# The order of the products in a split-float projection: PSUM tile by PSUM tile, lo part of the weights last

## The chip, the cores and the metric

The kernel runs on one core of a Trainium2 chip. The metric is device time in microseconds, from the first to the last instruction and the little that lies around them; the time given for a kernel is the median of its runs.

## The reference

One inference step of a decoder layer with two parallel branches, on a prompt of 1024 tokens and on 8 single sample tokens with 1024 cached positions each (1032 token columns in all, `NT`). Width is 1024, in 16 heads of 64.

```python
h = x * (1 + scale(c)) + shift(c)                       # adaLN
q, k, v, g_att, u, g_ssm, m_att, m_ssm = split(h @ w_in)   # 1024 x 8192
o = stick_breaking(q, k, v)        # A[t,s] = beta[t,s] * prod_{s<j<t} (1 - beta[t,j]), strictly causal
y = ssm(u)                         # 64 groups of 16 channels, 64 complex states each, scan over time
y = gelu(y + d_skip * u);  y = y * sigmoid(y @ w_glu + b_glu);  y_ssm = (y * silu(g_ssm)) @ w_ssm_out
y_att = (o * silu(g_att)) @ w_att_out
merged = sigmoid(m_att) * y_att + sigmoid(m_ssm) * y_ssm
x = LayerNorm(alpha * x + gate(c) * (merged @ w_out))
```

All is float32. Keys, values, final states and the new `x` are outputs.

## The kernel before, in words

**Projections.** Nearly all large products go through `gemm` (L124). An operand is held as two float32r tiles, `hi` (the rounded value) and `lo` (the rest). A projection takes one slab of weights (1024 inputs by 128 outputs) and makes 128 output rows for all 1032 token columns: three PSUM tiles `ps[0..2]` of 344 columns each (`c`), eight blocks of 128 inputs (`t`), three products for each (`i`): weights hi by activations hi, weights hi by activations lo, weights lo by activations hi. That is 72 matmuls (L141), each with its own weight load. The order before: for the first two and the last two values of `t` (`EDGE` is 2) tile by tile, three products for each `t`; for the four in between, at each `t` first the two products with the weights' hi part for all three tiles, then the three with the lo part. So a projection needs `wlo` for its third product, and its tiles end at products 60, 66 and 72. The next projection uses the same three PSUM buffers (`pj`, three of them; in the merge stage six) in the same order, and its first product in each waits until the former content has been copied out.

**Weights.** `Weights.emit` (L101) loads a slab (`w32`), rounds it on ScalarE (`whi`, L108) and subtracts on another engine (`wlo`, L109: VectorE in the first stages, POOL later). There are two buffers of each; the next slab is prepared when a projection takes its own.

**Stream.** `Stream` holds the queue of projections. `one` issues one matmul, and `weave` spreads them between the hand-ordered steps of the other work by a planned clock. `begin` and `head` start two projections ahead, while their operand is still being made. TensorE's order is thus written out by hand; the other engines' instructions are put in order by the scheduler of the framework, by priority and its own timing model, and each engine runs its queue in order. A projection's evacuation (`evac`) is written after its last matmul, one instruction for each of the three PSUM tiles.

**Stages.** (1) Modulation: `h` is made block by block, with the first two projections (`q` and `k` of pair 0) begun in between. (2) Attention, for eight pairs of heads: scores `z` (L654), sigmoids on ScalarE (L655, L656), a scan on VectorE (L665), transposes (L683) and values (L700), with four projections (`q`, `k`, `v`, gate) for the next pair woven in; `Attention.evac` copies out of PSUM into `z32` tiles (L574). (3) State space, for eight blocks of channels `f`: `matrices` (L936, L942), `inputs` (`sps`, L997; copied to `sr` and `si`, L999), the recurrence `recur` on VectorE (L1019 to L1037, result `xs`), `outputs` (`yp`, L1047 and L1048) and `gelu` (ScalarE L1080 to L1084, VectorE L1083 and L1085, the tanh at L1084 waiting for VectorE's L1083); three projections for each block are woven in, one `u` (copied out on ScalarE by `SSM.take`, L970) and two of the gates (`gate_evac`, L1520, and for the SSM gate also `zgate`, L1522). At the same time `SampleAttention` works through the cache of the sample tokens: indirect gathers on POOL (L807) of 2 MB tiles into `s_t`, multiply-adds on VectorE (`s_sc`, L828; values L823). Small VectorE copies (L805, L818, L815) from a recent tile (`k.last`: `u`, `sr`, `gin`, `gh`) pace them. (4) Merge: three chains of eight projections, `glu`, `ssm_out` and `att_out`, where each takes what the one before wrote (`act_g`, `act_s`, `act_a`); late values of the sample attention (`l_t`, L884, L885) run on VectorE beside them, their result `d_o` is needed by the transposes at L1285, and the projections of `att_out` follow. (5) `finish`: the output projection (L1397) and the LayerNorm.

Of the kernel before, what the change touches and what calls it, by code (L numbers as in the profile page):

```python
# [18 lines left out]
NC3, CW = 3, 344  # L19
KT = 8  # L20
# [57 lines left out]
def cs(c):  # L78
    return slice(CW * c, CW * c + CW)


def blk(i, w=128):
    return slice(w * i, w * i + w)
# [37 lines left out]
        return w  # L121


def gemm(k, act, evac, pre):  # L124


    PE = k.nc.tensor
    if pre:
        pre()
    whi, wlo = k.w.get()  # L130
    k.pj.append(k.pj.pop(0))
    ps = [k.pj[0].tile([128, 512], F32, tag="pj", bufs=NC3, name="pj")[:, 0:CW] for _ in range(NC3)]
    a = act() if callable(act) else act
    three = [(c, i) for c in range(NC3) for i in range(2)] + [(c, 2) for c in range(NC3)]
    ends = lambda ts: [(t, c, i) for c in range(NC3) for t in ts for i in range(3)]
    order = ends(range(EDGE)) + [(t, c, i) for t in range(EDGE, KT - EDGE) for c, i in three]
    order += ends(range(KT - EDGE, KT))
    for n, (t, c, i) in enumerate(order):
        ahi, alo = a[t]
        w, x = ((whi, ahi), (whi, alo), (wlo, ahi))[i]  # L140
        PE.matmul(ps[c], w[:, blk(t)], x[:, cs(c)], start=(t == 0 and i == 0), stop=(t == KT - 1 and i == 2))  # L141
        if n == len(order) - 1:
            evac(ps)
        yield


class Stream:
# [5 lines left out]
        self.clock = 0.0  # L153
        self.begun = deque()

    def add(self, act, evac, pre=None):
        self.jobs.append((act, evac, pre))
        self.left += KT * 9 * MM

    def later(self, ns, fn):  # L160
# [6 lines left out]
    def begin(self, n):  # L167

        for _ in range(n):
            self.begun.append([gemm(self.k, *self.jobs.popleft()), 0])  # L170

    def head(self, n):

# [7 lines left out]
    def one(self):  # L181

        if self.cur is None and self.begun:
            self.cur, self.n = self.begun.popleft()
        if self.cur is None:
            if not self.jobs:
                return False
            self.cur, self.n = gemm(self.k, *self.jobs.popleft()), 0
        next(self.cur)
        self.n += 1  # L190
        self.left -= MM
        self.clock += MM
        last = self.n == KT * 9
        if last:
            self.cur = None
            self.k.w.ensure()
        self.due()
        return None if last else True
# [32 lines left out]
def split_act(k, pool, src):  # L231
    hi = pool.tile([128, NT], F32R, tag="hi", bufs=KT, name="ahi")
    lo = pool.tile([128, NT], F32R, tag="lo", bufs=KT, name="alo")
    k.nc.scalar.copy(hi, src)
    k.nc.vector.tensor_tensor(lo, src, hi.bitcast(F32), ALU.subtract)  # L235
    return hi, lo
# [953 lines left out]
class Merge:  # L1190
# [33 lines left out]
    def glu(self):  # L1224
        k, nc = self.k, self.k.nc
        DVE, ACT = nc.vector, nc.scalar
        self.s_guard = self.pool("sets", "left")
        ps = self.s_guard.__enter__()
        self.act_s, held = [], {}

        def pre(f):
            g = self.ld.tile([128, NT], F32, tag="x", bufs=2, name="g")
            hi, lo = self.act_g[f]
            nc.gpsimd.tensor_tensor(g, hi.bitcast(F32), lo.bitcast(F32), ALU.add)
            s = self.load(k.d_sg[f], "m")
            (nc.gpsimd if GS == "p" else DVE).tensor_tensor(s, g, s, ALU.mult)
            held[f] = s

        def evac(f, p):
            g = held.pop(f)  # L1240
            for c in range(NC3):
                t = self.ld.tile([128, 512], F32, tag="sig", bufs=2, name="sig")[:, 0:CW]
                ACT.activation(t, p[c], AF.Sigmoid, bias=self.bg[:, f:f + 1])
                DVE.tensor_tensor(g[:, cs(c)], g[:, cs(c)], t, ALU.mult)
            self.act_s.append(split_act(k, ps, g))
            k.late.pace(g)

        for f in range(KT):
            k.stream.add(self.act_g, lambda p, f=f: evac(f, p), lambda f=f: pre(f))

    def ssm_out(self):
        k, nc = self.k, self.k.nc
        held = {}

        def pre(f):
            held[f] = self.load(k.d_mm[f], "m")

        def evac(f, p):
            m = held.pop(f)
            for c in range(NC3):  # L1260
                nc.vector.tensor_tensor(m[:, cs(c)], p[c], m[:, cs(c)], ALU.mult)
            k.q["P"].dma_start(k.d_pa[f], m)
            k.late.pace(m)

        for f in range(KT):
            k.stream.add(self.act_s, lambda p, f=f: evac(f, p), lambda f=f: pre(f))

    def open_a(self):

# [21 lines left out]
    def att_out(self):  # L1291
        k, nc = self.k, self.k.nc
        DVE = nc.vector
        self.m_guard = self.pool("setm", "left")
        pm = self.m_guard.__enter__()
        k.act_m, held = [], {}

        def pre(f):
            held[f] = self.load(k.d_ma[f], "m"), self.load(k.d_pa[f], "x")

        def evac(f, p):
            m, a = held.pop(f)
            for c in range(NC3):
                DVE.tensor_tensor(m[:, cs(c)], p[c], m[:, cs(c)], ALU.mult)
            DVE.tensor_tensor(m, m, a, ALU.add)
            k.act_m.append(split_act(k, pm, m))

        for f in range(KT):
            k.stream.add(lambda: self.act_a, lambda p, f=f: evac(f, p), lambda f=f: pre(f))

    def open_gate(self):
        k, io, ld = self.k, self.io, self.ld
# [406 lines left out]
```

## Time and profile before

| what | value |
|---|---|
| median of 3 runs | 1613.56 us (1612.72 to 1615.05) |
| the profiled execution | 1617.42 us, its span 1615.7 us |
| mean granted TensorE clock in it | 0.969 |
| matmuls, of these in projections (L141) | 9321, 6336 |
| start of the state-space stage, of the merge's first products | about 713 us, about 1172 us |
| projections done, start of the output products | 1504.5 us |

In the profile, PE is TensorE's matmuls and PEld its weight loads, DVE is VectorE, ACT ScalarE, POOL GpSimd, SP the queue that issues most DMAs. L141 is line 141 of the kernel. A row of waits reads: who waited <- for whom: microseconds in total, how often, the longest. In a timeline, a bracket at the end of a row is the idle time before that instruction and what ended it. The ends of matmuls are modelled; pace is read from their starts.

### The profile page before, as it was taken

To read this page: it belongs to the slowest core of one execution; us is meant where nothing else is said; L and a number is where in the kernel's file an instruction comes from. 1 tells how busy PE (TensorE), PEld (TensorE's weight loads), DVE (VectorE), ACT (ScalarE), POOL (GpSimd) and SP (SyncE) were. 2 spreads that over 40 slices of the span, in tenths; PEclk is the share of its full clock that TensorE was granted. 3 is DMA by queue.
4 is the path that set the end of the run, shared out by engine and by line. 5 is a ranking of instruction groups with operands and counts; after the bars stand their busy time and mean duration, and the time that the engine had idled before them with its cause. 6 is when DMAs were issued, how large, how long until landed. Compare 5 with 4: busy or idle time off the path is not lost.

```text
span 1615.7 us, 25524 instructions
## 1 busy us (share of the span) xinstructions
PE 1489.5 (92%) x9321; PEld 1410.2 (87%) x9321; DVE 1218.9 (75%) x1717; ACT 736.5 (46%) x1360; POOL 911.0 (56%) x744
## 2 busy tenths in 40 slices
PE   8899999999999999999989978889979786999997
PEld 4789999999999998999888978889779685899885
DVE  5558888888888888743899978787489975744566
ACT  3557777777776776643433333333432212311200
POOL 1738787878777877766566555552176541132164
PEclk9899999999999999999999989999989997999999
DMA  9323433334343434348789887875546677954322
GB/s 356 111 82 89 104 100 97 99 97 113 87 113 93 115 88 111 101 123 288 246 266 287 265 265 249 285 235 132 164 158 222 213 249 261 348 180 140 118 79 91
DMA packets 176731, 275.47 MB, mean 170 GB/s; under 512 B 46395, under 2 KB 119867, under 8 KB 176477
## 3 DMA queue, kind: packets, MB, share of 16 engines
q1 hardware_dynamic: 150555, 180.40, 36.6%
q0 software_dynamic: 23456, 84.95, 16.4%
q10 hardware_dynamic: 2594, 8.49, 2.0%
q8 instruction: 73, 1.20, 0.3%
q14 instruction: 53, 0.43, 0.1%
HBM read 196.77 MB, written 66.24 MB: 163 GB/s over the span
## 4 chain that ended last, share of the span: by engine, by line
PE 49%; DVE 26%; DMA 9%; issue 5%; ACT 3%; POOL 2%; SPq 1%; DVEq 0%; ACTq 0%; POOLq 0%
PE pj L141 32%; PE f L1397 6%; DVE s_sc L828 4%; PE o L700 3%; PE z L654 3%; PE tp L683 3%; DVE ke L665 3%; DVE l_t L884 2%; DMA s_t<-in_cache_k,s_idx 2%; DVE be L666 2%; DVE vs L636 2%; DMA l_t<-in_cache_v,l_idx 2%; DVE l_acc L885 2%; DVE wlo L109 1%; DVE xs L1037 1%
## 5 line engine op out<-in xcount | busy, mean ns | idle before, releaser
L141 PE MATMUL pj<-ahi,whi 128*128 128x344 f32 x2112 | 695.4, 331 | 36.8 <-ACT u L970 17.5
L141 PE MATMUL pj<-alo,whi 128*128 128x344 f32 x2112 | 686.1, 326 | 7.9 <-DVE alo L1220 4.1
L141 PE MATMUL pj<-ahi,wlo 128*128 128x344 f32 x2112 | 581.6, 328 | 6.0 <-POOL wlo L109 6.0
L141 PEld LDWEIGHTS pj<-ahi,whi 128*128 128x128 f32 x2112 | 405.6, 192 | 45.9 <-ACT u L970 18.3
L141 PEld LDWEIGHTS pj<-alo,whi 128*128 128x128 f32 x2112 | 405.6, 192 | 11.9 <-DVE alo L235 4.9
L141 PEld LDWEIGHTS pj<-ahi,wlo 128*128 128x128 f32 x2112 | 382.6, 192 | 8.0 <-POOL wlo L109 6.5
L665 DVE TENSOR_TENSOR_SCAN ke<-ke,eye 128x896 f32<-128x896 f32 (+7 forms) x128 | 217.7, 1701 | 92.4 <-ACT ke L655 92.2
L109 POOL TENSOR_TENSOR wlo<-w,whi 128x1024 fp32r<-128x1024 f32 x53 | 141.6, 2672 | 207.7 <-ACT whi L108 178.8
L108 ACT CAST whi<-w 128x1024 fp32r<-128x1024 f32 x90 | 94.9, 1055 | 137.3 <-PE pj L141 100.1
L655 ACT ACTIVATE ke<-z,nhb 128x448 f32<-128x448 f32 (+2 forms) x192 | 111.8, 582 | 81.1 <-PE z L654 79.2
L666 DVE TENSOR_TENSOR be<-be,ke 128x896 f32<-128x896 f32 (+7 forms) x128 | 128.0, 1000 | 13.0 <-ACT wthi L686 0.5
L828 DVE SCALAR_TENSOR_TENSOR s_sc<-s_t,s_q,s_sc 128x512 f32<-128x512 f32 x126 | 114.0, 905 | 18.0 <-DMA s_t<-in_cache_k,s_idx 12.0
L656 ACT ACTIVATE be<-z,hb 128x448 f32<-128x448 f32 (+2 forms) x192 | 110.6, 576 | 0.0
L807 POOL DMA_INDIRECT s_t<-in_cache_k,s_idx x64 | 70.6, 1103 | 50.8 <-DVE s_sc L828 15.5
L683 PE MATMUL tp<-ident,be 128*128 128x128 f32 x576 | 88.9, 272 | 0.0
L493 POOL TENSOR_TENSOR pt<-tab 128x256 f32<-128x256 f32 x64 | 79.5, 1241 | 3.1
L492 POOL TENSOR_TENSOR pr<-tab 128x256 f32<-128x256 f32 x32 | 25.9, 811 | 89.4 <-DMA tab<-d_tab 78.7
L1520 ACT ACTIVATE gate<-pj 128x344 f32<-128x344 f32 x72 | 32.7, 458 | 95.4 <-PE pj L141 86.5
L109 DVE TENSOR_TENSOR wlo<-w,whi 128x1024 fp32r<-128x1024 f32 x37 | 62.5, 1689 | 15.4 <-ACT whi L108 15.3
L686 ACT CAST wthi<-tp 128x512 fp32r<-128x512 f32 x96 | 56.7, 590 | 32.3 <-PE tp L683 29.9
L654 PE MATMUL z<-kl,qs 128*128 128x448 f32 (+2 forms) x192 | 66.0, 344 | 4.0 <-DMA kl<-kl 4.0
L687 DVE TENSOR_TENSOR wtlo<-tp,wthi 128x512 fp32r<-128x512 f32 x96 | 65.3, 680 | 5.7 <-ACT wthi L686 5.7
(314 smaller groups left out, 2758.5 us busy)
## 6 DMA issues: line engine op xcount, KB each, us to landing
w<-in_w_in SPq DMA_DIRECT2D x38, 512.0 KB
w<-in_w_in POOLq DMA_DIRECT2D x26, 512.0 KB, 5.6
wc<-in_w_cond SPq DMA_DIRECT2D x24, 512.0 KB
d_a<-ox SPq DMA_DIRECT2D x128, 64.0 KB
gst<-d_gg SPq DMA_DIRECT2D x8, 576.0 KB
x<-in_xr SPq DMA_DIRECT2D x9, 512.0 KB
xt<-in_xt SPq DMA_DIRECT2D x8, 516.0 KB
d_sg<-gate SPq DMA_DIRECT2D x8, 516.0 KB
```

The source lines that it names most:

```text
L108: nc.scalar.copy(whi, w32)
L109: self.eng.tensor_tensor(wlo, w32, whi.bitcast(F32), ALU.subtract)
L141: PE.matmul(ps[c], w[:, blk(t)], x[:, cs(c)], start=(t == 0 and i == 0), stop=(t == KT - 1 and i == 2))
L493: POOL.tensor_tensor(t1, c, d, ALU.mult)
L654: nc.tensor.matmul(z[:, 0:wide], st["q", h][:, blk(i)], x[:, s:s + wide], start=j == 0, stop=j == 1)
L655: nc.scalar.activation(ke[:, s:s + cw], z[:, 0:cw], AF.Sigmoid, bias=k.nhb[:, hd:hd + 1], scale=-0.125)
L656: nc.scalar.activation(be[:, s:s + cw], z[:, 0:cw], AF.Sigmoid, bias=k.hb[:, hd:hd + 1], scale=0.125)
L665: nc.vector.tensor_tensor_scan(rev, rev, self.eye[:, NP - n:][:, ::-1], 0.0, ALU.mult, ALU.add)
L666: nc.vector.tensor_tensor(be, be, ke[:, 1:n + 1], ALU.mult)
L683: PE.transpose(tp[:, 2 * order[a] + e], w[e][:, blk(2 * j + a)], k.ident)
L828: DVE.scalar_tensor_tensor(sc, t, q[:, d - d0:d - d0 + 1], sc, op0=ALU.mult, op1=ALU.add)
L1397: PE.matmul(pp[c], a[:, token(i)], w[:, blk(c, 512)], start=(t == 0 and a is ah and w is wh), stop=(t == KT - 1 and a is al))
```

## The change

`gemm` gets a further argument, `fresh`. Without it, the order is: for each of the three PSUM tiles in turn, the sixteen products with the weights' hi part over all eight `t`, then the eight with the lo part. With it, the order is the former one. Fresh are the two projections that `begin` starts in the modulation, and the first (`f == 0`) of `glu`, `ssm_out` and `att_out`. All other projections (attention from `v` of pair 0 on, `u`, the gates, seven of eight in each merge chain) take the new order. The number of matmuls, their operands and their place among the other steps are the same.

```diff
-def gemm(k, act, evac, pre):
+def gemm(k, act, evac, pre, fresh):
...
     order = ends(range(EDGE)) + [(t, c, i) for t in range(EDGE, KT - EDGE) for c, i in three]
     order += ends(range(KT - EDGE, KT))
+    if not fresh:
+        order = [(t, c, i) for c in range(NC3) for part in ((0, 1), (2,)) for t in range(KT) for i in part]
     for n, (t, c, i) in enumerate(order):
...
-    def add(self, act, evac, pre=None):
-        self.jobs.append((act, evac, pre))
+    def add(self, act, evac, pre=None, fresh=False):
+        self.jobs.append((act, evac, pre, fresh))
...
-            self.begun.append([gemm(self.k, *self.jobs.popleft()), 0])
+            self.begun.append([gemm(self.k, *self.jobs.popleft()[:3], True), 0])
...
-            k.stream.add(self.act_g, lambda p, f=f: evac(f, p), lambda f=f: pre(f))
+            k.stream.add(self.act_g, lambda p, f=f: evac(f, p), lambda f=f: pre(f), f == 0)
...
-            k.stream.add(self.act_s, lambda p, f=f: evac(f, p), lambda f=f: pre(f))
+            k.stream.add(self.act_s, lambda p, f=f: evac(f, p), lambda f=f: pre(f), f == 0)
...
-            k.stream.add(lambda: self.act_a, lambda p, f=f: evac(f, p), lambda f=f: pre(f))
+            k.stream.add(lambda: self.act_a, lambda p, f=f: evac(f, p), lambda f=f: pre(f), f == 0)
```

## The prediction

> **What bounds the kernel now.** The profiled execution took 1617.42 us (span 1615.7); the median of the three plain runs is 1613.56, so terms counted in its trace are taken off the median. Two times closer than about 0.2% (3.2 us) can't be told apart here. I read the page's busy shares first, then TensorE's waits, then busy time by stage, then the timelines around the longest waits.
>
> ```profile
> PE 1489.5 (92%) x9321; PEld 1410.2 (87%) x9321; DVE 1218.9 (75%) x1717; ACT 736.5 (46%) x1360; POOL 911.0 (56%) x744
> ...
> PE pj L141 <- ACT u L970: 17.5, 4, 8.7
> PE otp L1285 <- DMA orow<-d_o: 17.2, 1, 17.2
> PE yp L1048 <- DVE xs L1037: 9.9, 4, 3.5
> PE pj L141 <- POOL wlo L109: 6.0, 2, 3.1
> PE pj L141 <- ACT gate L1520: 4.2, 1, 4.2
> PE pj L141 <- ACT z L574: 2.4, 1, 2.4
> PE pj L141 <- ACT zgate L1522: 1.1, 1, 1.1
> ```
>
> TensorE is 92% busy. Of what it waits for, the change can touch two things: a PSUM tile that ScalarE has not yet copied out (`u`, `gate`, `zgate`: 17.5 + 4.2 + 1.1 = 22.8 us) and the weights' lo part (6.0 us). The 2.4 us behind `z` is the start of the third projection, behind the two begun ones, which keep their order; it stays. Now busy time by stage (columns: stretch, its length, PE, PEld, DVE, ACT, POOL busy, granted clock, DMA share, GB/s):
>
> ```profile
> 808.00:841.80 33.80, 28.87 (x187) 27.28 (x185) 32.06 (x56) 11.34 (x23) 22.64 (x18) 0.95 0.77 241
> 841.80:888.10 46.30, 43.18 (x288) 41.78 (x288) 45.19 (x92) 17.02 (x34) 31.65 (x31) 1.00 0.93 302
> 888.10:940.00 51.90, 43.19 (x288) 41.79 (x288) 43.53 (x84) 17.03 (x34) 29.39 (x30) 0.94 0.87 283
> 940.00:989.00 49.00, 44.88 (x288) 43.75 (x288) 39.87 (x79) 17.05 (x34) 26.21 (x26) 0.95 0.76 244
> 989.00:1026.50 37.50, 33.34 (x204) 32.03 (x204) 35.75 (x72) 13.16 (x24) 19.37 (x18) 0.91 0.80 247
> 1087.40:1143.00 55.60, 50.02 (x281) 43.19 (x281) 35.40 (x81) 16.96 (x34) 14.89 (x11) 0.91 0.54 138
> 1181.00:1347.00 166.00, 132.26 (x782) 130.31 (x782) 147.50 (x166) 33.62 (x45) 88.98 (x51) 0.89 0.66 219
> 1347.00:1504.50 157.50, 153.37 (x929) 149.58 (x930) 85.85 (x98) 37.53 (x38) 34.96 (x12) 0.98 0.66 224
> ```
>
> All of the 22.8 us lie in the state-space stage, one per channel block. There VectorE is as full as TensorE (45.19 of 46.30 us and 32.06 of 33.80, but 39.87 of 49.00 later), and the DMA engines are 76 to 93% busy. In the merge, 1181 to 1347, VectorE has 147.50 of 166 us. Only after 1347 is TensorE alone the bound, with hardly a wait. So an idle microsecond of TensorE is worth a microsecond only where VectorE too stands still for it.
>
> **The change, part by part.** *Number and pace of products.* None is added or dropped: 72 in each projection in both orders. The new order puts 24 in a row into one PSUM tile. Rows that bound this: 600 in the old mixed order, and, in the last token block, 24 in a row into one tile of 512 columns against the interleaved tiles before it (columns: PE, PEld).
>
> ```profile
> 1410.07 94.46 PE pj L141 x600
> ...
> 1543.90:1554.90 11.00, 11.00 (x49) 8.85 (x49) 1.00 0.42 145
> 1593.90:1604.90 11.00, 11.00 (x49) 8.72 (x47) 1.00 0.14 52
> ```
>
> 94.46 / 600 = 157 ns each; and 49 products in 11 us either way, so the row of one tile costs nothing.
>
> *PSUM release.* Before, the three tiles end at products 60, 66 and 72, and the next projection rewrites each 12 products later: 12 x 0.157 = 1.9 us. After, they end at 24, 48 and 72 and are rewritten 48 products later, 7.5 us. A copy may be 5.6 us later than now without stopping TensorE. The longest case, in ScalarE's timeline, then TensorE's:
>
> ```profile
> 927.67 0.63 ACT L1084 ACTIVATE gq<-gq 128x512 f32<-128x512 f32 x1 [6.80 <-DVE gq L1083]
> 937.90 0.63 ACT L1084 ACTIVATE gq<-gq 128x512 f32<-128x512 f32 x1 [7.87 <-DVE gq L1083]
> 939.23 1.38 ACT L970 COPY u<-pj 128x344 f32<-128x344 f32 x2
> 940.39 1.07 ACT L108 CAST whi<-w 128x1024 fp32r<-128x1024 f32 x1
> ...
> 930.70 0.62 PE L997 MATMUL sps<-ug,gin 128*128 128x136 f32 x4
> 940.04 0.66 PE L141 MATMUL pj<-ahi,whi 128*128 128x344 f32 x1 [8.72 <-ACT u L970]
> ```
>
> The `u` copies stand behind two tanh that wait for VectorE. In the new order the first tile is done some 10 us before 930.7 (48 products, and a set of `yp` and one of `sps` between them), so about 921: its copy runs there, or right after the tanh of 927.67, both in time. The second is done about 926; if its copy falls behind the tanh of 937.90 it ends near 938.5 and is wanted at 930.9 + 24 x 0.157 + 0.45 = 935.1: a wait of at most 3.4 us in place of 8.7. The other five (1.1 to 4.2 us) are shorter than 5.6 and go. I take 22.8 - 1.7 (half of 3.4) = 21 us of TensorE waits removed.
>
> *What that is worth.* The clock after each wait, then VectorE's timeline in the same places:
>
> ```profile
> 940.00:944.30 4.30, 4.26 (x15) 0.50 0.75 250
> 944.30:948.60 4.30, 4.30 (x30) 0.99 0.53 154
> 888.10:891.50 3.40, 3.36 (x20) 1.00 1.01 267
> 989.00:992.20 3.20, 3.16 (x11) 0.51 1.03 382
> 1087.40:1091.00 3.60, 3.60 (x13) 0.55 0.96 268
> ...
> 838.93 0.69 DVE L1083 TENSOR_TENSOR gq<-gq,gh 128x512 f32<-128x512 f32 x1 [1.04 <-ACT gq L1082]
> 936.40 0.75 DVE L828 SCALAR_TENSOR_TENSOR s_sc<-s_t,s_q,s_sc 128x512 f32<-128x512 f32 x1 [5.46 <-DMA s_t<-in_cache_k,s_idx]
> 946.64 0.15 DVE L805 COPY s_t<-sr 128x1 f32<-128x1 f32 x1 [0.61 <-ACT sr L999]
> 950.57 0.69 DVE L1020 TENSOR_TENSOR gq<-sr,es 128x512 f32<-128x512 f32 x1 [3.78 <-ACT sr L999]
> 996.39 2.29 DVE L838 TENSOR_TENSOR_SCAN s_ke<-s_ke,zcol 128x1024 f32<-128x1024 f32 x1 [1.22 <-ACT s_ke L835]
> 1093.88 0.15 DVE L815 COPY s_acc<-sr 128x1 f32<-128x1 f32 x1 [2.91 <-ACT sr L999]
> 1098.58 0.69 DVE L823 SCALAR_TENSOR_TENSOR s_t<-s_t,s_sc 128x512 f32<-128x512 f32 x1 [3.81 <-DMA s_t<-in_cache_v,s_idx]
> ```
>
> After the waits of 8.7, 4.1 and 4.2 us TensorE ran at half clock for 4.3, 3.2 and 3.6 us: another 2.2 + 1.6 + 1.6 = 5.4 us of its time (after the 3.1 us one it stayed at 1.00). So up to 28 us of TensorE's time comes free. But the stage is handed on by VectorE's recurrence (L1019 to L1037), and VectorE stood still for TensorE only in these rows: 1.0 us at 838.9; 0.6 + 3.8 at 946 and 950, where `sr` waited for `sps` products stuck behind the 8.7 us; 1.2 at 996; 2.9 at 1093.9, of which I count nothing, since at 1098.6 it waits for a gather anyway. Sum 1.0 + 4.4 + 1.2 = 6.6, rounded to 7 with a little from the 2.9. The rest comes back as waits of `yp` for `xs`, 9.9 us now.
>
> *The lo part last.* The first product that needs `wlo` moves from third to seventeenth: 14 x 0.157 = 2.2 us. The two waits, 6.0 us together, shrink to about 1.6. Both lie in the merge before 1347, where VectorE is full and the 17.2 us wait for `d_o` follows: that wait grows by what is saved. Worth 0 at the end; if the cover were gone, 4.4.
>
> *Queues.* No DMA issue is moved. The `whi` buffer is last read at product 64 instead of 71, so the next cast on ScalarE, and the POOL subtraction with the gathers queued behind it, may start up to 1.1 us earlier; POOL's subtraction still waits for the old `wlo`, whose last use stays at 72. I count 0, between 0 and -1. The first copy writes its SBUF tile (`z32`, `gate`, `uu`) 5.6 us earlier; if the former content still has to go out, the copy stands at the head of ScalarE's queue and holds what is behind it (third rival).
>
> *Fresh projections.* The two begun at the start and the first of each merge product keep their order: 0.
>
> Sum: -7 us of 1613.56, that is 1606.5. It lies nearer VectorE's 6.6 than TensorE's 28 because the stage's own rows show VectorE at 95 to 98% in two of the stretches.
>
> **The rivals.** *First: TensorE sets the end after all.* The chain that ended last:
>
> ```profile
> PE 49%; DVE 26%; DMA 9%; issue 5%; ACT 3%; POOL 2%; SPq 1%; DVEq 0%; ACTq 0%; POOLq 0%
> ...
> 939.23 0.77 ACT u L970
> ```
>
> TensorE has half of it, the `u` copy of the longest wait stands on it, and earlier `sps` let gathers (paced on `sr` and `u`) start earlier too. Then all 28 us count, perhaps less one or two: 1587. Against it stand 45.19 of 46.30 us and the DMA share of 0.93.
>
> *Second: nothing moves.* Either VectorE and the gathers take up everything (at 936.40 it waits 5.46 us for a gather that no PSUM tile delays), or the copies stay where they are, behind the tanh, so that the first tile is still free only at 939.9. ScalarE's rows show it working strictly in order: `u` at 939.23 had been ready for 8 us. The Trainium skill says the same, in "TensorE: Matmul & The Clock Gate", Part 1: ScalarE and VectorE are strict first in, first out; by that rule a tile done earlier is free earlier only if its copy is queued earlier, and the trace agrees. Time 1613.5.
>
> *Third, slower: the earlier copies hold ScalarE in the attention stage.* There ScalarE already stands at copies whose products are not done:
>
> ```profile
> ACT z L574 <- PE pj L141: 16.2, 22, 2.0
> ```
>
> That is 0.74 us each time, for tiles that end close together. With tiles 24 products apart, two more copies in each of some 28 projections may stand like this: 28 x 2 x 0.74 = 41 us of ScalarE time, in front of the sigmoids that feed VectorE's scans. ScalarE has slack, so I let a third arrive: +14, 1627. It decides from 0.12 us per added stop that reaches the end (7 us over 56).
>
> The Trainium skill has a rule for the clock as well ("TensorE: Matmul & The Clock Gate", Part 1): an idle window of about 3.4 us halves it. The rows agree (1.00 after 3.1 us, 0.50 to 0.55 after 4.1 and more). By it the removed waits also bring back the half-clock stretches, which are in the first rival's 28 us.
>
> **How the numbers follow.** Forecast, 4 to 14 us faster: 0.50. First rival, 1582 to 1599: 0.13. Second: 0.22. Third: 0.15. Faster by over 0.2% (below 1610.3): 0.50 + 0.13 less 0.03 at the forecast's edge = 0.60; within: 0.25; slower: 0.15. The predicted time is the forecast's, 1606.5; its own range is 1599 to 1610. The range for 8 in 10 leaves out the far half of the first rival and of the third: 1593 to 1619.
>
> **What would show it.** Right: in TensorE's waits `u`, `gate` and `zgate` fall from 22.8 us to under 5, `wlo` from 6.0 to under 2, `yp <- xs` grows above 9.9, the wait for `d_o` stays or grows; products still come every 157 ns; the first `u` copy stands ahead of a tanh in ScalarE's timeline; the handover near 1143 comes about 7 us earlier, and from there to the end the trace is as long as before. Wrong: the waits gone and the handover 20 us earlier (first rival), or the waits still there (second), or the attention stage, 90 to 713, longer by more than 3 us (third).

## The result and the profile after

The changed kernel takes 1632.85 us (median of 4 runs, 1631.98 to 1637.48) beside 1614.3 us for the kernel before on the same chip (1612.72 to 1617.32): a ratio of 1.0118, 95% interval 1.0096 to 1.0139. It is slower by about 19 us, where the forecast was 7 us faster. The two profiled executions differ by less, 14.6 us (spans of 1615.7 and 1630.3), because the one before was some 3 us above its median.

In the changed file all line numbers behind `gemm` are three higher: L144 is the product of a projection, L569 the copy `zg`, L609 the subtraction `kl`, L657 the score product, L1051 `yp`. First the steps of the two profiled executions (us, from marks read off TensorE's timeline: first projection product, last score `z`, first transpose of the state space, last `ysp`, first `otp`, first `f`, end), with four of the experiments beside them:

| step | before | after | `gold` | `klvec` | `gvec` | `gvec_before` |
|---|---|---|---|---|---|---|
| attention stage | 676.2 | 704.1 | 674.3 | 658.1 | 660.8 | 656.8 |
| handover to the state space | 34.0 | 41.5 | 42.4 | 41.8 | 35.0 | 35.2 |
| state space | 409.9 | 395.4 | 395.9 | 394.3 | 396.3 | 405.9 |
| merge, to `otp` | 204.2 | 198.9 | 201.7 | 197.9 | 198.4 | 201.3 |
| merge, to `f` | 157.2 | 155.6 | 154.9 | 153.9 | 153.7 | 153.7 |
| rest | 111.4 | 111.4 | 111.4 | 111.4 | 111.4 | 111.4 |

The change did shorten the stages it was costed in: state space by 14.5 us, merge by 5.3 + 1.6. It lengthened the two steps ahead of them, attention by 27.9 and the handover by 7.5. TensorE's waits after (the columns are who waits for whom, total us, times, longest):

```profile
PE z L657 <- ACT be L659: 35.6, 7, 5.6
PE yp L1051 <- DVE xs L1040: 19.0, 6, 7.8
PE otp L1288 <- DMA orow<-d_o: 11.5, 1, 11.5
PE pj L144 <- POOL wlo L109: 7.1, 2, 5.5
PE pj L144 <- ACT gate L1523: 5.2, 1, 5.2
PE pj L144 <- ACT zgate L1525: 1.2, 1, 1.2
```

The `u` waits (17.5 us) are gone. The new first row is a score product that waits 5 us for ScalarE's sigmoid, seven times: once in each pair of heads but the first. The row in which `zg` occurs before, and then what ScalarE itself waited for after:

```profile
POOL sg L567 <- ACT zg L566: 57.8, 8, 23.6
```

```profile
ACT zg L569 <- POOL kl L609: 32.4, 7, 5.1
ACT zgate L1525 <- POOL gate L1527: 6.1, 1, 6.1
ACT z L577 <- PE pj L144: 9.6, 22, 0.5
```

Before, `zg` appears as something that others wait for, and no row has it waiting. After, it waits seven times for `kl`, which neither feeds it nor is fed by it. The reason is a buffer. `zg` takes its SBUF tile from the tag `z32`, whose three buffers go round as q, k, v, `sg`, `zg`, so `zg` lands in the buffer that holds this pair's keys. Their second half is still to be read by POOL's `kl`, which is held back until the scores of the former pair are out. ScalarE's timeline at the second pair, then POOL's, then TensorE's:

```profile
169.08 0.47 ACT L568 ACTIVATE sg<-pj 128x344 f32<-128x344 f32 x1
174.32 0.45 ACT L569 COPY zg<-pj 128x344 f32<-128x344 f32 x1 [4.77 <-POOL kl L609]
174.66 0.69 ACT L658 ACTIVATE ke<-z,nhb 128x512 f32<-128x512 f32 x1
...
169.58 1.47 POOL L495 TENSOR_TENSOR pi<-tab 128x256 f32<-128x256 f32 x1
171.01 0.80 POOL L496 TENSOR_TENSOR pt<-tab 128x256 f32<-128x256 f32 x1
171.89 2.40 POOL L609 TENSOR_TENSOR kl<-z,kh 64x1024 fp32r<-64x1024 f32 x1
...
175.99 0.80 PE L657 MATMUL z<-kh,qs 128*128 128x512 f32 x1 [5.24 <-ACT be L659]
```

`zg`'s wait of 4.77 us ends when `kl` is done; the sigmoid `ke`, which has nothing to do with either, stands behind it and starts only at 174.66; TensorE waits 5.24 us for the sigmoids' PSUM tiles. The same place before, ScalarE then POOL:

```profile
169.59 0.69 ACT L655 ACTIVATE ke<-z,nhb 128x512 f32<-128x512 f32 x1 [0.39 <-PE z L654]
180.08 0.46 ACT L565 ACTIVATE sg<-pj 128x344 f32<-128x344 f32 x1
180.42 0.45 ACT L566 COPY zg<-pj 128x344 f32<-128x344 f32 x1
...
169.63 3.13 POOL L606 TENSOR_TENSOR kl<-z,kh 64x1024 fp32r<-64x1024 f32 x1
```

`kl` ended 1.5 us earlier then (172.76 against 174.29), still later than 169.55, where `zg` began to wait after the change; `zg` came 8 us after it had ended. In this stage the products of a projection are woven between other work, so "36 products earlier" is not 5.6 us but 11 us (180.08 against 169.08).

The wait costs more than its length. TensorE's clock behind it (stretch, length, PE, PEld, DVE, ACT, POOL busy, granted clock):

```profile
175.99:179.30 3.31, 3.31 (x12) 3.12 (x13) 2.42 (x3) 2.40 (x5) 2.72 (x4) 0.50 0.72 166
179.30:184.00 4.70, 4.70 (x31) 4.39 (x31) 4.00 (x5) 2.74 (x7) 0.00 (x0) 0.85 0.70 172
```

The granted clock stays at half up to 180.74, for 4.75 us. Behind the seven waits such stretches are 2.8 to 6.2 us long, 32.4 us in all, and TensorE is busy throughout them: a loss of at most 16.2 us. Over the same 600 us of the attention stage, before and after:

```profile
90.00:690.00 600.00, 581.43 (x3946) 567.35 (x3946) 505.64 (x480) 427.18 (x860) 440.81 (x375) 1.00 0.38 100
```

```profile
90.00:690.00 600.00, 563.62 (x3753) 552.24 (x3753) 460.49 (x457) 413.10 (x820) 410.70 (x360) 0.96 0.36 95
```

TensorE is idle for 581.43 - 563.62 = 17.8 us more, not for the whole 35.6 us of new waits, because its waits for VectorE in this stretch fell at the same time, from 17.6 us to 0.8. With the half clock that is at most 34 us. Counted by work, the 193 matmuls fewer are 29 us at the former pace of 600 us for 3946; the stage grew by 27.9.

The handover repeats it with another reader. The gates begun there use `z32` too, and the second waits for POOL's multiplication of the first, which stands behind the table products. After, ScalarE then POOL:

```profile
739.00 0.45 ACT L1525 COPY zgate<-pj 128x344 f32<-128x344 f32 x1 [6.10 <-POOL gate L1527]
...
735.93 0.72 POOL L497 TENSOR_TENSOR pi<-pi,pt 128x256 f32<-128x256 f32 x1
736.61 2.35 POOL L1527 TENSOR_TENSOR gate<-gate,zgate 128x1032 f32<-128x1032 f32 x1
```

### The profile page after: what moved, and what is told of

It is laid out like the page before. It is cut to its first block, busy times and chain, and to the rows that moved or that the text cites. A ratio compares the mean times of both kernels' runs of the same rounds, so it can differ in the third digit from the quotient of the medians.

```text
span 1630.3 us, 25533 instructions
## 1 busy us (share of the span) xinstructions
PE 1496.3 (92%) x9321; PEld 1420.3 (87%) x9321; DVE 1191.8 (73%) x1717; ACT 747.1 (46%) x1360; POOL 892.6 (55%) x744
## 4 chain that ended last, share of the span: by engine, by line
PE 53%; DVE 16%; DMA 10%; POOL 9%; issue 5%; ACT 2%; SPq 1%; DVEq 0%; POOLq 0%; ACTq 0%
PE pj L144 35%; PE f L1400 6%; DVE s_sc L831 5%; PE o L703 3%; PE z L657 3%; PE tp L686 3%; POOL pt L496 2%; DMA out_k_p<-sv 2%; DMA s_t<-in_cache_k,s_idx 2%; POOL pr L497 1%; DMA l_t<-in_cache_v,l_idx 1%; POOL kl L609 1%; DVE xs L1040 1%; DMA d_g<-yy 1%; DMA sga<-d_sa 1%
## 5 line engine op out<-in xcount | busy, mean ns | idle before, releaser
L144 PE MATMUL pj<-ahi,whi 128*128 128x344 f32 x2112 | 694.2, 332 | 18.7 <-ACT ahi L237 9.0
L144 PE MATMUL pj<-alo,whi 128*128 128x344 f32 x2112 | 683.9, 327 | 9.4 <-DVE alo L1223 4.0
L144 PEld LDWEIGHTS pj<-ahi,whi 128*128 128x128 f32 x2112 | 407.6, 193 | 26.6 <-ACT ahi L237 9.5
L144 PE MATMUL pj<-ahi,wlo 128*128 128x344 f32 x2112 | 420.9, 326 | 7.1 <-POOL wlo L109 7.1
L144 PEld LDWEIGHTS pj<-alo,whi 128*128 128x128 f32 x2112 | 407.5, 193 | 13.9 <-DVE alo L238 6.7
L144 PEld LDWEIGHTS pj<-ahi,wlo 128*128 128x128 f32 x2112 | 349.1, 191 | 9.4 <-POOL wlo L109 7.6
L668 DVE TENSOR_TENSOR_SCAN ke<-ke,eye 128x896 f32<-128x896 f32 (+7 forms) x128 | 213.0, 1664 | 62.8 <-ACT ke L658 62.6
L109 POOL TENSOR_TENSOR wlo<-w,whi 128x1024 fp32r<-128x1024 f32 x53 | 133.0, 2510 | 225.2 <-PE pj L144 125.1
L831 DVE SCALAR_TENSOR_TENSOR s_sc<-s_t,s_q,s_sc 128x512 f32<-128x512 f32 x126 | 111.5, 885 | 14.6 <-DMA s_t<-in_cache_k,s_idx 13.0
L657 PE MATMUL z<-kh,qs 128*128 128x448 f32 (+2 forms) x192 | 68.4, 356 | 35.6 <-ACT be L659 35.6
L810 POOL DMA_INDIRECT s_t<-in_cache_k,s_idx x64 | 70.1, 1095 | 54.2 <-DVE s_q L821 14.6
L570 POOL TENSOR_TENSOR sg<-sg,zg 128x1032 f32<-128x1032 f32 x8 | 24.1, 3018 | 102.0 <-ACT zg L569 102.0
L495 POOL TENSOR_TENSOR pr<-tab 128x256 f32<-128x256 f32 x32 | 31.7, 990 | 85.4 <-DMA tab<-d_tab 72.3
```

What stands on the lines that cost most here:

```text
L109: self.eng.tensor_tensor(wlo, w32, whi.bitcast(F32), ALU.subtract)
L657: nc.tensor.matmul(z[:, 0:wide], st["q", h][:, blk(i)], x[:, s:s + wide], start=j == 0, stop=j == 1)
L668: nc.vector.tensor_tensor_scan(rev, rev, self.eye[:, NP - n:][:, ::-1], 0.0, ALU.mult, ALU.add)
L831: DVE.scalar_tensor_tensor(sc, t, q[:, d - d0:d - d0 + 1], sc, op0=ALU.mult, op1=ALU.add)
```

## The experiments

Theory A: an evacuation that comes early writes an SBUF buffer that POOL has still to read, and holds ScalarE's queue. Rivals: every early copy costs ScalarE by itself (theory B), or TensorE's long rows into one PSUM tile disturb the stage (theory C). All of these ran beside the kernel before; its median was 1617.0 us beside `gold`, `only_g`, `only_qkv` and `klfirst`, 1613.1 beside `klvec`, `best`, `only_ssm` and `only_merge`, 1612.2 beside `klvec_before`, `klvec_tile` and `gvec`, and 1613.8 beside `gvec_before`.

**Attention's gate in the former order, all else new (`gold`).**

```diff
-            S.add(k.act_h, lambda ps, kind=kind: box[0].evac(p, kind, ps))
+            S.add(k.act_h, lambda ps, kind=kind: box[0].evac(p, kind, ps), None, kind == "g")
```

> The changed kernel, but the attention gates (kind g, once per pair) keep the former order. Theory A: the loss is the early copy zg, which takes the z32 buffer that still holds the keys, and stands at the head of ScalarE's queue until POOL's subtraction kl has read them; then the seven waits of z for the sigmoids be (35.6 us) and the half clock after them go, the attention stage is as long as before within 3 us, and with the gain of the later stages the time is about 1596 (1591 to 1602). Theory B: the loss is that every earlier copy (q, k, v, g) holds ScalarE while its products are not done; then about a quarter of the 36 us goes, and the time is 1620 to 1626. Theory C: the long rows of one PSUM tile themselves disturb the attention stage; 1620 to 1630.

Measured: 1607.09 us, ratio 0.9939 (0.9923 to 0.9956). Eight projections of the kernel make the difference between slower and faster, and the time is below what theories B and C gave (1620 and more). TensorE's wait for the sigmoids falls from 35.6 us to this row:

```profile
PE z L657 <- ACT be L659: 4.7, 3, 2.4
```

The number forecast, 1596, was missed: the handover stays at 42.4 us, which the forecast had let go with the rest, and the merge is 2.8 us longer than after the change.

**Only attention's gate new (`only_g`), and only q, k and v of attention new (`only_qkv`).** The same argument of `add` is set to `kind != "g"` or `kind == "g"`, and to `True` in all other projections.

> The former order everywhere, except the attention gates (kind g), which take the new one. Theory A: the whole loss of the attention stage is here, 32 to 37 us: 1646 to 1652. Theory B: a quarter of it: 1622 to 1626. Theory C: a quarter: 1620 to 1626.

> The former order everywhere, except q, k and v of the attention stage, which take the new one. Theory A: within 3 us of the kernel before, 1611 to 1617, or a little below, as short waits for late VectorE work may change. Theory B: three quarters of the loss, 1638 to 1644. Theory C: the same, 1635 to 1644.

Measured: 1636.27 us, ratio 1.0120 (1.0103 to 1.0137), and 1620.98 us, 1.0021 (1.0001 to 1.0040). The eight gate projections alone bring a loss as large as the whole change's, though without its gains: their attention stage is 699.3 us, which is 23.1 of the 27.9 us. With q, k and v alone it is 675.2 us, no longer than before, where theories B and C gave three quarters of the loss; the whole is 0 to 6 us slower. The size that theory A gave for the gates was 10 us too large. With the gates alone, `zg` waits:

```profile
ACT zg L569 <- POOL kl L609: 22.9, 7, 3.9
```

**The subtraction `kl` with a higher priority (`klfirst`).** The POOL instruction is put under `high_priority(HURRY)`.

> The changed kernel with one edit: the subtraction kl on POOL gets the same high priority as the copies out of PSUM, so that it goes ahead of the table products in POOL's queue; all orders of products stay new. Theory A: kl ends some us earlier, the key's z32 buffer is free when zg comes, the wait of zg for kl (32.4 us) falls below 8 us, and the time is 1597 to 1608. Theories B and C: no change, 1628 to 1637.

Measured: 1634.13 us, ratio 1.0105 (1.0082 to 1.0128). It decides nothing, since the edit did not move the instruction. POOL's timeline, with the table product still ahead:

```profile
172.51 0.80 POOL L496 TENSOR_TENSOR pt<-tab 128x256 f32<-128x256 f32 x1
173.39 2.40 POOL L610 TENSOR_TENSOR kl<-z,kh 64x1024 fp32r<-64x1024 f32 x1
```

**The subtraction `kl` on VectorE, new order throughout (`klvec`).**

```diff
-        nc.gpsimd.tensor_tensor(kl[own], z[own, 0:NP], kh[own].bitcast(F32), ALU.subtract)
+        nc.vector.tensor_tensor(kl[own], z[own, 0:NP], kh[own].bitcast(F32), ALU.subtract)
```

> The order after throughout, but the subtraction that makes the keys' lo part (kl) runs on VectorE instead of POOL, so that it no longer stands behind POOL's table products. Theory A: the copy zg then waits below 8 us for kl over the stage (32.4 after), TensorE's waits of z for ScalarE's be fall from 35.6 to below 12 us, the attention stage falls from 704 to about 682 us, and the time to 1606 to 1616 us; VectorE does some 14 more subtractions of 1 to 1.3 us, which can cost up to 9 us of this. Rival B (the early copy costs ScalarE by itself, whoever reads the buffer): attention stays above 698 us and the time above 1627 us.

Measured: 1586.78 us, ratio 0.9852 (0.9824 to 0.9879): 46 us less than after the change by the medians, 43 by the ratios, by moving the one instruction that `zg` waited for. The row of `zg` waiting for `kl` is gone, `zg` runs where its product ends, and TensorE hardly stands:

```profile
PE z L657 <- ACT be L659: 3.5, 8, 1.0
```

```profile
167.59 0.47 ACT L568 ACTIVATE sg<-pj 128x344 f32<-128x344 f32 x1
167.94 0.46 ACT L569 COPY zg<-pj 128x344 f32<-128x344 f32 x1
```

The early copy doesn't hold ScalarE by itself: the rival, an attention stage above 698 us, is refuted. But the attention stage is 658.1 us, 18 us shorter than before the change, and the time 19 us below the 1606 to 1616 forecast; theory A doesn't give that. So the next run takes the order away again.

**The former order with `kl` on VectorE (`klvec_before`).**

> The former order everywhere, with the subtraction kl on VectorE: the order is the one difference to the kernel that has kl on VectorE and the new order (1586.8 us; its attention stage 658, handover 42, state space 394, the two merge steps 198 and 154). Theory A with a separate gain of moving kl (the new order is worth +7.5 us at the handover, -14.5 in the state space, -5 in the merge, nothing in the attention stage once POOL doesn't read the buffer late): attention 656 to 663 us, total 1595 to 1603. Rival F (the attention stage needs the new order for its 658 us): attention 670 to 677 us, total 1608 to 1616.

Measured: 1588.35 us, ratio 0.9853 (0.9833 to 0.9874). The attention stage is 655.5 us, and the total is 7 us below the range that theory A gave: most of the gain of `klvec` is the moved subtraction's own, in either order. It also leaves the new order worth nothing that can be told (1586.78 against 1588.35): by the profiles, its state space is 12.4 us shorter (394.3 against 406.7) and its merge 3.7, but its handover is 7.7 longer, its attention stage 2.6, the last part of its merge 1.8, and its first product starts 3.1 us later.

**The state-space gates.** In `best`, attention's gates and the state-space gates of kind g keep the former order (the argument of `add` is `s == "g"`); `kl` stays on POOL. In `gvec`, all is new, `kl` is on VectorE, and so is the gate's multiplication:

```diff
-            nc.gpsimd.tensor_tensor(t, t, z, ALU.mult)
+            nc.vector.tensor_tensor(t, t, z, ALU.mult)
```

> The order after, but the eight projections of the attention's own gate and the eight state-space gates whose second copy feeds a POOL product (kind g) keep the former order. Theory A (an early copy into an SBUF buffer that POOL still has to read holds ScalarE): the step from the last scores to the first transpose of the state space, 42.4 us when only the attention's gate keeps the former order, falls back to about 34 us, the waits of zgate for POOL fall from 18.8 us to below 8, and the rest stays: 1599 us (1594 to 1604). Rival D (the handover is long because the u copies come early, not the gates): the step stays near 42 us and the time near 1607 us.

> kl on VectorE, the new order, and the multiplication of the state-space gate by its sigmoid on VectorE instead of POOL, so that the buffers of the three gates made at the handover come free without POOL's table products ahead. Theory A at the second place: the handover falls from 41.8 to 34 to 37 us, ScalarE's waits for POOL's gate (17.2 us) go. Whether the time follows: 1577 to 1582 us if those 6 us last, 1584 to 1589 us if the merge stage gives them back, as it did where the gates alone went back to the former order.

Measured: `best` 1607.61 us, ratio 0.9973 (0.9957 to 0.9989); `gvec` 1581.74 us, ratio 0.9809 (0.9787 to 0.9831). In both the handover falls as theory A says, 42.4 to 34.9 and 41.8 to 35.0 us, so its place is confirmed twice, once by a later copy and once by an earlier reader; `best` also refutes rival D, since its `u` copies still come early. Only `gvec` keeps the gain: the time of `best` is no better than `gold`'s and missed its forecast of 1599. In `best` the merge takes 208.8 us instead of `gold`'s 201.7, with these waits there (`gold` has 14.1 us for `d_o`):

```profile
PE otp L1288 <- DMA orow<-d_o: 17.8, 1, 17.8
PE pj L144 <- POOL wlo L109: 11.8, 4, 6.3
```

Why the merge gave it back in one and not in the other was not settled. `gvec` is the fastest version of all, 50 us below the changed kernel.

**The former order with both operations on VectorE (`gvec_before`).**

> The former order everywhere, with both POOL operations that read the shared buffers (kl and the gate's multiplication) on VectorE: beside the kernel with both on VectorE and the new order (1581.7 us; handover 35, state space 396, merge 198 and 154) it gives what the order by itself is worth once nothing holds the early copies. My forecast's arithmetic (some 20 us of waits removed, most given back as waits for VectorE, a net of 7 us): 1586 to 1591 us. Rival H (the multiplication on VectorE brings the 5 to 6 us whatever the order): 1580 to 1584 us, and the order is worth nothing.

Measured: 1590.08 us, ratio 0.9845 (0.9821 to 0.9870). Against `gvec` the order is now worth 8.3 us by the medians and 5.8 us by the ratios (0.0036 of 1614); the two intervals overlap by 0.001, so a small gain is likely rather than sure. In the former order the multiplication on VectorE brings nothing (1590.08 against 1588.35), so what `gvec` gained over `klvec` (5 us by the medians, 6.8 in the handover) goes to the collision. TensorE's waits, `gvec_before` then `gvec`:

```profile
PE otp L1285 <- DMA orow<-d_o: 16.8, 1, 16.8
PE pj L141 <- ACT u L970: 15.3, 3, 7.3
PE yp L1048 <- DVE xs L1037: 7.1, 4, 2.4
```

```profile
PE yp L1051 <- DVE xs L1040: 19.0, 6, 6.5
PE otp L1288 <- DMA orow<-d_o: 10.0, 1, 10.0
```

15.3 us of waits for `u` go, and 11.9 us come back as waits of `yp` for VectorE's recurrence.

**The stages one at a time (`only_ssm`, `only_merge`).** Only the state space's u and gate projections new; only the merge's three.

> The former order in all of the attention's and the merge's projections, the new one in the u and gate projections of the state space alone. Theory A: attention as before (676 us), handover 41.5 instead of 34.0 us, state space near 395 instead of 410 us, merge as before: 1607 to 1611 us on a chip where before takes 1615. Rival E (the state space's gain comes out of the time that the attention stage lost, as work that was done there earlier): the state-space step stays above 404 us and the time is 1619 to 1625 us.

> The former order everywhere but in the three projections of the merge stage (their first tile row each keeps its own setting). If the merge's gain of 5 us in the order after is its own: 1609 to 1612 us where before takes 1615, with the step between the state space's output and the last output transpose near 199 us instead of 204. If it comes from what the state-space stage left undone or done: 1614 to 1616 us and 203 to 205 us.

Measured: 1606.4 us, ratio 0.9963 (0.9947 to 0.9978), with a state space of 395.6 and a handover of 40.9 us; and 1613.76 us, ratio 1.0015 (1.0002 to 1.0029), with a merge of 207.7 us to `otp`. The state space's gain and the handover's loss both belong to the state-space projections. The merge step is longer than either forecast for it (199, or 203 to 205). The merge's 5 us after the change are not the merge order's own.

**The lo part not last (`klvec_tile`).** `klvec`, tile by tile, but the three products of each block together.

```diff
-        order = [(t, c, i) for c in range(NC3) for part in ((0, 1), (2,)) for t in range(KT) for i in part]
+        order = [(t, c, i) for c in range(NC3) for t in range(KT) for i in range(3)]
```

> kl on VectorE and one PSUM tile at a time, but the three products of each block stay together, so that the weights' lo part is wanted at product 3 and not at product 17. If lo last is worth nothing, as my step (c) had it: 1583 to 1591 us, TensorE's waits for wlo 6 to 10 us against 6.9. Rival G (lo last hides the making of wlo): waits for wlo above 14 us and more than 1593 us.

Measured: 1593.51 us, ratio 0.9872 (0.9845 to 0.9899). The time is half a microsecond inside rival G's, but its interval overlaps that of `klvec`, and the waits for `wlo`, 11.0 us in four against 6.9 in two, lie between the two forecasts. By the medians lo last is worth 6.7 us, by the ratios 3.2, and by the intervals it can't be told from nothing; this stays open.

## Why the prediction was wrong

**The step that failed** is the last sentence but one under *Queues*: "I count 0, between 0 and -1. The first copy writes its SBUF tile (`z32`, `gate`, `uu`) 5.6 us earlier; if the former content still has to go out, the copy stands at the head of ScalarE's queue and holds what is behind it". The hazard was named and then put at nothing in the sum, without a look at who still reads each buffer; the third rival, to which it was passed on, prices copies that wait for their products. It cost 28 us in attention and 7.5 us at the handover. The rows to price it were in the trace before: `kl` ends at 172.76 (169.63 + 3.13) and `zg` came at 180.42, so 7.7 us were in hand, and the move is 11 us. Two further errors are in that sentence: the distance was taken at the back-to-back pace of 157 ns a product, which doesn't hold where projections are woven with other work; and the content had not to "go out" but to be read by another engine.

**The third rival** had the direction, the stage and nearly the time (1627), and its sign, an attention stage longer by more than 3 us, is what came. So much was luck, because its mechanism is refuted: it had copies standing for products that weren't done, and that row fell from 16.2 to 9.6 us.

**PSUM release** was right as far as it went: `u` is gone, `zgate` stays at 1.2 us against the 5 us in all that were allowed, but one wait for `gate` of 5.2 us remains, 6.4 us in all. There ScalarE's copy stands behind a sigmoid that waits 8.44 us for VectorE:

```profile
1021.80 1.15 ACT L838 ACTIVATE s_ke<-s_sc,s_bias 128x1024 f32<-128x1024 f32 x1 [8.44 <-DVE s_sc L831]
1023.77 0.46 ACT L1523 ACTIVATE gate<-pj 128x344 f32<-128x344 f32 x1
```

**What that is worth.** Forecast -7; with the collisions taken away, -5.8 to -8.3. That fits the term in sum, and the return of about half of the removed waits as `yp` waiting for `xs` (9.9 to 19.0 us) has the sign as written. By stage it doesn't fit, so the agreement of the sum is partly luck: the state space alone gave 14.5 us after the change and 9.6 in `gvec`, and the stages around it took some back (attention is 4.0 us longer in `gvec` than in `gvec_before`).

**The lo part last.** Forecast: the waits fall from 6.0 to about 1.6 us. They are 7.1, because one of them is 5.5 us long and no order of 2.2 us covers it: POOL makes that `wlo` at 1283.33, behind gathers that waited for VectorE. That the wait for `d_o` would stay or grow was wrong too, 17.2 to 11.5 us.

```profile
1280.01 1.75 POOL L869 DMA_INDIRECT l_t<-in_cache_v,l_idx  x1 [1.85 <-DVE l_t L868]
1283.33 2.35 POOL L109 TENSOR_TENSOR wlo<-w,whi 128x1024 fp32r<-128x1024 f32 x1
```

**Second rival.** The rule cited with it, strict order on ScalarE from "TensorE: Matmul & The Clock Gate", Part 1 of the Trainium skill, was used for PSUM alone. The trace agrees with it, at 4.77 us in the row above, and it speaks against any copy that is moved ahead of its buffer's last reader, in SBUF as well.

## What to carry to other kernels

An evacuation that is moved earlier needs two things free: its PSUM tile and the buffer it writes into. For each, list the last reader, its engine and what is queued ahead of it, and compare the slack with the move in time as the trace has it at that place, not in instructions. When a reorder loses, see which instruction waits at the head of a queue and for whom: here, with its releaser moved to another engine, one instruction a head, the order that had cost 19 us cost nothing (1586.78 against 1588.35 us). What the move gained beyond that it gained in either order.

## What the runs showed of the hardware

Moving `kl` from POOL to VectorE was expected to cost VectorE up to 9 us. It made the attention stage shorter than before the change, by 18.1 us with the new order (`klvec`) and by 20.7 us with the former one (`klvec_before`). VectorE's busy time did not grow: 1218.9 us with 1717 instructions before, and in `klvec_before`:

```profile
PE 1484.1 (94%) x9321; PEld 1407.0 (89%) x9321; DVE 1211.3 (76%) x1733; ACT 735.4 (46%) x1360; POOL 864.5 (55%) x728
```

The same subtraction lasts 2.9 us in the mean on POOL and 1.6 us on VectorE, and another VectorE subtraction, `vs`, became shorter. The groups of the stage, before and then `klvec_before`:

```profile
L606 POOL TENSOR_TENSOR kl<-z,kh 64x1024 fp32r<-64x1024 f32 x14 | 40.9, 2923 | 1.0
L636 DVE TENSOR_TENSOR vs<-sv,vs 128x256 fp32r<-128x256 f32 x32 | 36.2, 1171 | 0.0
```

```profile
L606 DVE TENSOR_TENSOR kl<-z,kh 64x1024 fp32r<-64x1024 f32 x14 | 21.8, 1559 | 0.9 <-ACT kh L604 0.2
L636 DVE TENSOR_TENSOR vs<-sv,vs 128x256 fp32r<-128x256 f32 x32 | 23.8, 782 | 0.0
```

The mean of `vs` before hides two kinds. Its shortest, median and longest time in ns, before and then after the change:

```profile
L636 DVE TENSOR_TENSOR vs<-sv,vs x32: 417/842/2634, 101.4 to 637.6; 128x256 fp32r<-128x256 f32 x32
```

```profile
L639 DVE TENSOR_TENSOR vs<-sv,vs x32: 418/839/959, 102.2 to 664.0; 128x256 fp32r<-128x256 f32 x32
```

Before, seven of the 32 take 2.6 us and the others at most 0.90. The seven are just those that begin while POOL works on `kl`, and each ends 0.28 to 0.29 us after `kl` does: the first of them begins at 170.42 and ends at 173.04, beside the `kl` of 169.63 to 172.76. The traces of `gold`, `best`, `only_g`, `only_qkv`, `only_ssm` and `only_merge` have seven such cases each, with the same 0.28 to 0.29 us. After the change `kl` is still on POOL, but no `vs` begins within it, and none is long. So this VectorE subtraction stands until POOL's is over.

"SBUF — State Buffer", section "SBUF: two separate sides", of the Trainium skill says that VectorE and GpSimd share one pair of ports under an exclusive lock, so that an operation of the one can block the other for a whole instruction. The 49 cases agree with that.

TensorE's waits for VectorE from 90 to 690 us, before and then `klvec_before`:

```profile
PE tps L614 <- DVE wtlo L687: 7.3, 7, 1.1
PE o L700 <- DVE wdlo L687: 7.0, 5, 1.5
PE o L700 <- DVE wtlo L687: 3.3, 7, 0.5
```

```profile
PE o L700 <- DVE wtlo L687: 1.3, 3, 0.4
PE o L700 <- DVE wdlo L687: 0.6, 1, 0.6
```

They fall from 17.6 to 1.9 us, 15.7 of the 20.7 us that the stage became shorter. That the end of the collisions is what took them away is argued, not shown: no run kept `kl` on POOL, out of the way of `vs`, without TensorE standing elsewhere.
